# Up projection of a gated MLP: the convolution's sum in PSUM, the gelu further back in ScalarE's queue, the residual on every second tile

## The chip, the cores and the metric

The kernel runs on one core of a Trainium2 chip. The metric is the device time of one execution in microseconds. Engines are named as in the profile: PE is TensorE (PEld its weight loads), DVE is VectorE, ACT is ScalarE, POOL is GpSimd, SP is SyncE, which here only issues transfers. PSUM has eight banks of 128 x 512 fp32; matmuls write there, and DVE and ACT can read and write there too.

## The reference, cut to what matters

One decoder layer on 512 tokens of width 2048: attention heads of four kinds, an output projection, a layer norm, and a gated MLP with a second layer norm. The change concerns the MLP's first half:

```python
def conv_ffn(x, w_up, conv_w, conv_b, w_down):
    S = x.shape[1]
    u, g = jnp.split(x @ w_up, 2, axis=-1)
    gp = jnp.pad(g, ((0, 0), (CONV_WIDTH - 1, 0), (0, 0)))
    gc = conv_b
    for tap in range(CONV_WIDTH):
        gc = gc + conv_w[tap] * gp[:, tap:tap + S]
    return (jax.nn.gelu(gc) * u) @ w_down
...
    h = layer_norm(DEEPNORM_ALPHA * h + mix, ln1_g[l], ln1_b[l])
    ffn = conv_ffn(h, ffn_w_up[l], ffn_conv_w[l], ffn_conv_b[l], ffn_w_down[l])
    h = layer_norm(DEEPNORM_ALPHA * h + ffn, ln2_g[l], ln2_b[l])
```

The hidden width is 5632, that is 44 tiles of 128 hidden columns (f = 0 to 43), each with 512 tokens on the free axis.

## The kernel before

Everything is fp32, and each product is made from three matmuls on rounded parts (high x high, high x low, low x high, in the code `PARTS`). The up projection (`ffn_up`) multiplies blocks in Strassen's manner with seven products: a tile f takes two **units** of weights (u = 0 and 1, each half of the 2048 rows), and a unit is 7 products x 4 blocks x 3 parts = 84 matmuls of 128 x 256. A tile's results lie in four PSUM banks `bk[0..3]`; even tiles take three banks of a ring of three and one of a ring of five, odd tiles four of the ring of five. Tile 0 is made in another way, and the last two tiles take their units in another order.

Each unit's operands are prepared ahead of PE by `weight_operands`, called by `next_unit`:

- SP loads the raw weights `wr` (L918, two transfers of 512 KB, four buffers).
- ACT writes `wl` = -raw (L925) and `wh` = rounded raw (L928). `wh` and `wl` have two buffers each, so both wait until PE has done the first three of the seven products of the unit two before.
- POOL issues an accumulating transfer (L926, 768 KB) that adds the raw weights from memory to `wl`, which leaves raw minus rounded. PE needs `wl` at the very start of the unit.
- POOL makes four sums of blocks, `S` (L934 to L937); ACT rounds each (L899) and DVE takes the rest (L900, the pair in `split_pair`). PE needs these `ws` from the fourth product on.

Once a tile's second unit is through, `up_finish` (L988 on) collects the banks: ACT copies `bk[0]`, whose first half alone is used (L995), DVE makes the gate `g` and the other half `up` (L996 to L1002). `gated` then makes the convolution: ACT the last tap and the bias (L1010), DVE the two others (L1011, L1013) into an SBUF tile `c`, ACT the gelu in place (L1015), POOL the product with `up` (L1016). After every odd tile `set_aside` has POOL make three or four half sums `ht` (L1031 to L1036) and SP store all to memory. Once a tile, on 16 tiles in a row (f = 2 to 17), `up_residual` loads a piece of the first norm's output, multiplies and adds on DVE (L1054, L1055), and stores it for the end of the down projection.

The order of the instructions on each engine is set at compile time by a scheduler from the order of the code and from priorities: all of `weight_operands` is moved ahead by a priority of 900. On the chip each engine takes its instructions strictly in that order, and so does SP with its transfers. SBUF temporaries (`tmp`) come from a ring of 36.

Of the kernel before, what the change touches and what calls it, by code (L numbers as in the profile page):

```python
# [13 lines left out]
AF = mybir.ActivationFunctionType  # L14
# [7 lines left out]
NT = S // P  # L22
NMEM = 256
DFF = 5632
FT = DFF // P
# [16 lines left out]
class Trunk:  # L42
    def __init__(self, ctx, tc, x, memt, wfg, wm, wmkv, wout, wup, wdown, wtail, w1, prm, rows,
                 out):
        self.tc, self.nc = tc, tc.nc
        self.x, self.memt, self.wfg, self.wm, self.wmkv = x, memt, wfg, wm, wmkv
        self.wout, self.wup, self.wdown, self.wtail, self.w1 = wout, wup, wdown, wtail, w1
        self.prm_d, self.rows, self.out = prm, rows, out
        pool = lambda name, bufs, **kw: ctx.enter_context(tc.tile_pool(name=name, bufs=bufs, **kw))
        self.pT = pool("pT", 16)  # L50
        self.pW = pool("pW", 3)
        self.pP = pool("pP", 2)
        self.pt = pool("pt", 36)
        self.sm = pool("sm", 3)
        self.cst = pool("cst", 1)
        self.ps = pool("ps", 4, space=bass.MemoryType.PSUM)
        self.dram = pool("dram", 1, space=bass.MemoryType.DRAM)
        self.wm_next = 0

        self.queue = deque()  # L60
        self.stage_b, self.stage_c = deque(), deque()
        self.phase = 0
        self.every, self.count = 24, 0
        self.late = deque()
        self.ahead = 0
        self.unit, self.unit_no = None, 0

# [828 lines left out]


    def split_pair(self, raw, h, l):
        self.nc.scalar.copy(h, raw)  # L899
        self.nc.vector.tensor_sub(l, raw, h.bitcast(F32))  # L900

    def next_unit(self):

        w = self.unit
        self.unit = self.weight_operands(self.units.popleft()) if self.units else None
        self.unit_no += 1
        return w

    def weight_operands(self, src):

        nc = self.nc
        with self.tc.high_priority(offset=900 if self.unit_no > 1 else 200):
            raw = [self.pW.tile([P, 2, 512], F32, tag="wr", name="wr", bufs=4) for _ in range(2)]
            for p in range(2):
                nc.sync.dma_start(raw[p], src[:, 2 * p:2 * p + 2])  # L918
            a21, a11 = raw[0][:, 0], raw[0][:, 1]
            a12 = raw[1][:, 0]  # L920
            a22 = raw[1][:, 1]
            h3, l3 = (self.pW.tile([P, 3, 512], F32R, tag=g, name=g, bufs=2)
                      for g in ("wh", "wl"))
            for o, i in ((slice(0, 1), raw[0][:, 1:2]), (slice(1, 3), raw[1])):
                nc.scalar.mul(l3[:, o], i, -1.0)  # L925
            nc.gpsimd.dma_start(l3, src[:, 1:4], accum_op=ALU.add)  # L926
            for o, i in ((slice(0, 1), raw[0][:, 1:2]), (slice(1, 3), raw[1])):
                nc.scalar.copy(h3[:, o], i)  # L928
            if self.unit_no < 2:
                w = [self.tmp("w21", dt=F32R, tag="w") for _ in range(2)]  # L930
                self.split_pair(a21, *w)
                return [[h3[:, i], l3[:, i]] for i in range(3)] + [w]
            s12, s34 = (self.pP.tile([P, 2, 512], F32, tag="P", name="S") for _ in range(2))
            nc.gpsimd.tensor_add(s12[:, 0], a21, a22)  # L934
            nc.gpsimd.tensor_sub(s12[:, 1], s12[:, 0], a11)  # L935
            nc.gpsimd.tensor_sub(s34[:, 0], a11, a21)  # L936
            nc.gpsimd.tensor_sub(s34[:, 1], a12, s12[:, 1])  # L937
            ws = []
            for t in (s12, s34):
                for i in range(2):  # L940
                    ws.append([self.tmp("ws", dt=F32R, tag="w") for _ in range(2)])
                    self.split_pair(t[:, i], *ws[-1])
        return [[h3[:, i], l3[:, i]] for i in range(3)] + ws


# [42 lines left out]
    def up_finish(self, f, bk):  # L988
        nc = self.nc
        half = lambda ap: ap.rearrange("p (a n) -> p a n", a=2)  # L990

        pu = half(self.tmp("pu"))
        p1, u2 = pu[:, 0], pu[:, 1]
        g, uu = self.tmp("g"), self.tmp("uu", (P, 2, 256))
        nc.scalar.copy(p1, bk[0][:, :256])  # L995
        nc.vector.tensor_add(u2, p1, bk[1][:, 256:])  # L996
        nc.vector.tensor_add(g[:, :256], p1, bk[1][:, :256])
        nc.vector.tensor_add(uu, u2.unsqueeze(1).to_broadcast([P, 2, 256]), half(bk[2]))
        nc.vector.tensor_add(g[:, 256:], uu[:, 0], bk[3][:, :256])
        up = self.tmp("up")  # L1000
        nc.vector.tensor_add(up[:, :256], uu[:, 1], bk[3][:, 256:])
        nc.vector.tensor_add(up[:, 256:], uu[:, 1], bk[2][:, :256])  # L1002
        self.gated(f, g, up)

    def gated(self, f, g, up):

        nc = self.nc
        c = self.tmp("c")
        cw = lambda k: self.prm[:, C_CW + 44 * k + f:C_CW + 44 * k + f + 1]
        nc.scalar.activation(c, g, AF.Identity, bias=self.prm[:, C_CB + f:C_CB + f + 1], scale=cw(2))  # L1010
        nc.vector.scalar_tensor_tensor(c[:, 1:], g[:, :511], cw(1), c[:, 1:], op0=ALU.mult,  # L1011
                                       op1=ALU.add)
        nc.vector.scalar_tensor_tensor(c[:, 2:], g[:, :510], cw(0), c[:, 2:], op0=ALU.mult,  # L1013
                                       op1=ALU.add)
        nc.scalar.activation(c, c, AF.Gelu_apprx_tanh)  # L1015
        (nc.vector if f == 0 else nc.gpsimd).tensor_mul(c, c, up)  # L1016
        c = c.rearrange("p (a n) -> p a n", a=2)
        if f % 2 == 0:
            self.b1 = c
        else:  # L1020
            self.aside.append(self.set_aside(self.b1, c))
# [24 lines left out]
    def up_residual(self, i):  # L1046

        nc = self.nc
        n, t = divmod(i, NT)
        if t == 0:  # L1050
            self.gb1 = self.bc_row(2, n, "g1"), self.bc_row(3, n, "b1")
        a = self.tmp("res")
        nc.sync.dma_start(a, self.res[t][n])
        nc.vector.scalar_tensor_tensor(a, a, ALPHA, self.gb1[0], op0=ALU.mult, op1=ALU.mult)  # L1054
        nc.vector.scalar_tensor_tensor(a, self.gb1[1], ALPHA, a, op0=ALU.mult, op1=ALU.add)  # L1055
        self.res[t][n] = self.dram.tile([P, 512], F32, name=f"ares{t}{n}")
        nc.sync.dma_start(self.res[t][n], a)

# [108 lines left out]
    def ffn(self):  # L1169
        nc = self.nc  # L1170
# [3 lines left out]
        for f, u in self.up_sequence():  # L1174
            n = int(f in seen)
            seen.add(f)
            if f > 0:
                self.ffn_up(f, u, n)
            elif n:
                self.gated(f, *self.up_first())  # L1180
            if n and 2 <= f < 18:
                self.up_residual(f - 2)
        self.st2 = [self.cst.tile([P, 4, 6], F32, name=f"st2_{t}") for t in range(NT)]
        self.due = deque((4, 5))
        acc = []
# [1 line left out]
        for c, k0, nk in self.CHUNKS:  # L1187
            sets = self.column_sets(c)
            for q in sets:
                bk = [self.bank("g" if i < 3 else "a", "dn") for i in range(7)]  # L1190
                nu = nk // 2
                for u in range(nu):
                    w = self.next_unit()
# [26 lines left out]
        for f in range(2, 4):  # L1220
            h, l = self.load_unit(self.wtail[f])
            tail += [(h[:, k * 512:(k + 1) * 512], l[:, k * 512:(k + 1) * 512]) for k in range(2)]
        gb = [(self.bc_row(4, q, "g2"), self.bc_row(5, q, "b2")) for q in range(4)]
# [164 lines left out]
```

## Time and profile before

| | us |
|---|---|
| median of 3 runs | 2334.61 |
| lowest and highest | 2327.23, 2335.04 |
| the profiled execution | 2341.35 |
| its span, first to last instruction | 2339.6 |
| mean granted clock of PE, share of full speed | 0.983 |
| PE busy | 2232.7 |
| DVE, ACT, POOL busy | 1591.7, 1229.5, 1368.4 |

The up projection lies at 945 to 1815 us of the span, the down projection behind it. Busy time says how full an engine is, not whether it is waited for; for that the waits of PE are read by stretch, and then who held up the one that PE waited for.

### The profile page before, as it was taken

How to read it: one execution, taken by the hardware profiler on the slowest of the kernel's cores; microseconds unless marked ns; L12 is line 12 of the kernel's file. 1: busy time of each engine (PE TensorE's matmuls, PEld its weight loads, DVE VectorE, ACT ScalarE, POOL GpSimd, SP SyncE). 2: the span in 40 equal slices, each digit the busy share in tenths (PEclk: the TensorE clock that was granted, in tenths of full speed). 3: DMA queues.
4: the chain of work that ended last, by engine and by line, in shares of the span. 5: the costliest groups of instructions: out<-in, count | busy, mean ns of one | idle time of the engine just before them, and what ended most of it. 6: DMA issues, size and time to landing. Idle time of an engine off the chain costs nothing. (4 is left out here: it accounts for less than half of the span.)

```text
span 2339.6 us, 40306 instructions
## 1 busy us (share of the span) xinstructions
PE 2232.7 (95%) x15454; PEld 2083.5 (89%) x15454; DVE 1591.7 (68%) x2204; ACT 1229.5 (53%) x2129; POOL 1368.4 (58%) x1197
## 2 busy tenths in 40 slices
PE   7999999999999998899999999999999899999995
PEld 6788888888888878899999999999999899899994
DVE  7544455456675348687787767777676878677778
ACT  5444453355563135565555555565555666565651
POOL 5212110123234517787887878877777687777874
PEclk9999999999999999999999999999999999999998
DMA  6322223222124363888888777777778888788873
GB/s 228 92 81 73 78 67 106 84 64 62 59 88 149 104 188 94 224 226 227 231 222 238 202 210 207 201 204 197 212 202 227 243 241 233 193 229 216 207 191 115
DMA packets 125362, 392.75 MB, mean 168 GB/s; under 512 B 13632, under 2 KB 23744, under 8 KB 125168
## 3 DMA queue, kind: packets, MB, share of 16 engines
q1 hardware_dynamic: 106304, 287.72, 35.6%
q0 software_dynamic: 18720, 102.24, 24.6%
q8 instruction: 121, 1.98, 0.3%
q14 instruction: 73, 0.60, 0.1%
q10 hardware_dynamic: 144, 0.21, 0.0%
HBM read 354.36 MB, written 35.65 MB: 167 GB/s over the span
## 5 line engine op out<-in xcount | busy, mean ns | idle before, releaser
L900 DVE TENSOR_TENSOR ws<-S,ws 128x512 fp32r<-128x512 f32 x512 | 600.1, 1192 | 244.3 <-ACT ws L899 238.9
L963 PE MATMUL up<-xt,ws 128*128 128x256 f32 x3096 | 386.4, 283 | 0.3 <-DVE ws L900 0.3
L963 PEld LDWEIGHTS up<-xt,ws 128*128 128x128 f32 x3096 | 378.0, 192 | 0.6 <-DVE ws L900 0.6
L899 ACT CAST ws<-S 128x512 fp32r<-128x512 f32 x512 | 307.0, 615 | 114.9 <-POOL S L934 33.5
L100 DVE TENSOR_TENSOR wl<-wr,wh 128x1024 fp32r<-128x1024 f32 x122 | 155.2, 1272 | 213.3 <-ACT wh L99 198.4
L936 POOL TENSOR_TENSOR S<-wr 128x512 f32<-128x512 f32 x128 | 212.0, 1656 | 92.5 <-DVE ws L900 87.3
L342 POOL TENSOR_SCALAR P<-P,r 128x128 f32<-128x128 f32 (+3 forms) x144 | 81.1, 582 | 308.5 <-DVE r L337 166.2
L963 PE MATMUL up<-x,wh 128*128 128x256 f32 x1376 | 258.8, 288 | 0.0
L99 ACT CAST wh<-wr 128x1024 fp32r<-128x1024 f32 x122 | 128.0, 1049 | 233.7 <-PE op L733 78.8
L934 POOL TENSOR_TENSOR S<-wr 128x512 f32<-128x512 f32 x128 | 183.8, 1436 | 108.0 <-issue 45.3
L925 ACT ACTIVATE wl<-wr 128x512 fp32r<-128x512 f32 (+1 forms) x260 | 205.1, 836 | 67.3 <-PE dn L1115 43.5
L928 ACT CAST wh<-wr 128x512 fp32r<-128x512 f32 (+1 forms) x260 | 211.5, 829 | 35.7 <-PE up L963 33.8
L963 PE MATMUL up<-x,wl 128*128 128x256 f32 x688 | 200.8, 292 | 29.5 <-DMA wl<-in_wup_dram 29.3
L963 PEld LDWEIGHTS up<-x,wh 128*128 128x128 f32 x1376 | 220.5, 197 | 0.0
L937 POOL TENSOR_TENSOR S<-wr,S 128x512 f32<-128x512 f32 x128 | 211.8, 1655 | 0.0
L935 POOL TENSOR_TENSOR S<-S,wr 128x512 f32<-128x512 f32 x128 | 198.5, 1551 | 9.7
L1115 PE MATMUL dn<-wh,hx 128*128 128x256 f32 x792 | 157.5, 292 | 13.3 <-DVE acc L1128 8.6
L963 PEld LDWEIGHTS up<-x,wl 128*128 128x128 f32 x688 | 135.8, 197 | 33.7 <-DMA wl<-in_wup_dram 33.7
L1115 PEld LDWEIGHTS dn<-wh,hx 128*128 128x128 f32 x792 | 132.3, 200 | 14.9 <-issue 6.3
L733 PE MATMUL op<-wh,oTs 128*128 128x512 f32 x448 | 140.6, 391 | 0.0
L963 PE MATMUL up<-x,ws 128*128 128x256 f32 x1032 | 137.9, 283 | 0.0
L1015 ACT ACTIVATE c<-c 128x512 f32<-128x512 f32 x44 | 27.8, 632 | 208.0 <-DVE c L1013 208.0
(327 smaller groups left out, 5321.3 us busy)
## 6 DMA issues: line engine op xcount, KB each, us to landing
wr<-in_wup_dram SPq DMA_DIRECT2D x176, 512.0 KB
wl<-in_wup_dram POOLq DMA_DIRECT2D x88, 768.0 KB, 7.5
wr<-in_wm_dram SPq DMA_DIRECT2D x84, 512.0 KB
wr<-in_wdown_dram SPq DMA_DIRECT2D x84, 512.0 KB
wl<-in_wdown_dram POOLq DMA_DIRECT2D x42, 768.0 KB, 7.4
wr<-in_wout_dram SPq DMA_DIRECT2D x32, 512.0 KB
hid<-c SPq DMA_DIRECT2D x44, 256.0 KB
hid<-ht SPq DMA_DIRECT2D x44, 256.0 KB
```

What stands on the lines that cost most here:

```text
L100: nc.vector.tensor_sub(l[:, :cols], raw[:, :cols], h[:, :cols].bitcast(F32))
L733: nc.tensor.matmul(ps, ot[ct][:, a, t * P:(t + 1) * P], w[b][:, c2 * 512:(c2 + 1) * 512], start=(first and (a, b) == (0, 0)), stop=(last a ...
L899: self.nc.scalar.copy(h, raw)
L900: self.nc.vector.tensor_sub(l, raw, h.bitcast(F32))
L925: nc.scalar.mul(l3[:, o], i, -1.0)
L928: nc.scalar.copy(h3[:, o], i)
L934: nc.gpsimd.tensor_add(s12[:, 0], a21, a22)
L935: nc.gpsimd.tensor_sub(s12[:, 1], s12[:, 0], a11)
L936: nc.gpsimd.tensor_sub(s34[:, 0], a11, a21)
L937: nc.gpsimd.tensor_sub(s34[:, 1], a12, s12[:, 1])
L963: self.nc.tensor.matmul(ps, w[iw][i][:, k * P:(k + 1) * P], x[j][ix], start=(opens and k == 0 and (i, j) == (0, 0)), stop=(last and k == 3 ...
L1115: self.nc.tensor.matmul(bk[i][:, a * 256:(a + 1) * 256], x[ix][j][:, a * P:(a + 1) * P], w[iw][p][:, q * 256:(q + 1) * 256], start=first a ...
```

## The change

Three things, all in the up projection:

1. For f = 1 to 41 the convolution is summed in `bk[0]`, the bank that held the first product, and not in an SBUF tile. (For tile 0, 42 and 43 all stays as it was.)
2. For the same tiles the gelu, its product with `up` and what follows are put off to the next call of `next_unit` (`defer`, `run_deferred`), and the gelu is queued on ACT behind the last rounding of the unit prepared by that call (`issue_after(self.mark.ins)` orders the queue only). The gelu's result goes to a new SBUF tile.
3. `up_residual` runs on every second tile from f = 2 to 32, and each piece is loaded when the piece before has been stored.

```diff
     def split_pair(self, raw, h, l):
-        self.nc.scalar.copy(h, raw)
+        ins = self.nc.scalar.copy(h, raw)
         self.nc.vector.tensor_sub(l, raw, h.bitcast(F32))
+        return ins
+
+    def defer(self, units, work):
+        self.deferred.append((self.unit_no + units, work))
+
+    def run_deferred(self):
+        todo = [w for n, w in self.deferred if n < self.unit_no]
+        self.deferred = [d for d in self.deferred if d[0] >= self.unit_no]
+        with self.tc.issue_after(self.mark.ins):
+            for work in todo:
+                work()
 
     def next_unit(self):
 
         w = self.unit
         self.unit = self.weight_operands(self.units.popleft()) if self.units else None
         self.unit_no += 1
+        self.run_deferred()
         return w
...
-                    self.split_pair(t[:, i], *ws[-1])
+                    self.mark = self.split_pair(t[:, i], *ws[-1])
...
-        self.gated(f, g, up)
+        self.gated(f, g, up, bk[0] if f < FT - 2 else None)
...
-    def gated(self, f, g, up):
+    def gated(self, f, g, up, c=None):
         nc = self.nc
-        c = self.tmp("c")
+        if c is None:
+            c = self.tmp("c")
...
-        nc.scalar.activation(c, c, AF.Gelu_apprx_tanh)
+        if 0 < f < FT - 2:
+            self.defer(0, lambda: self.activate(f, c, up))
+        else:
+            self.activate(f, c, up)
+
+    def activate(self, f, s, up):
+        nc = self.nc
+        c = self.tmp("c") if 0 < f < FT - 2 else s
+        nc.scalar.activation(c, s, AF.Gelu_apprx_tanh)
         (nc.vector if f == 0 else nc.gpsimd).tensor_mul(c, c, up)
...
     def up_residual(self, i):
         nc = self.nc
+        def load(i):
+            n, t = divmod(i, NT)
+            gb = (self.bc_row(2, n, "g1"), self.bc_row(3, n, "b1")) if t == 0 else None
+            a = self.tmp("res")
+            nc.sync.dma_start(a, self.res[t][n])
+            return a, gb
         n, t = divmod(i, NT)
-        if t == 0:
-            self.gb1 = self.bc_row(2, n, "g1"), self.bc_row(3, n, "b1")
-        a = self.tmp("res")
-        nc.sync.dma_start(a, self.res[t][n])
+        a, gb = self.res_next if i else load(i)
+        self.gb1 = gb or self.gb1
...
         nc.sync.dma_start(self.res[t][n], a)
+        if i + 1 < 4 * NT:
+            self.res_next = load(i + 1)
...
-            if n and 2 <= f < 18:
-                self.up_residual(f - 2)
+            if n and 2 <= f < 34 and f % 2 == 0:
+                self.up_residual(f // 2 - 1)
```

How the queues move. ACT, in the middle of the up projection, from the last roundings of one unit to the copy of the next tile's first bank (L928, L925, L899 prepare units; L1010 is the first tap, L1015 the gelu, L995 the copy). Before:

```order
L1010 ACTIVATE c<-g,prm 128x512
L1015 ACTIVATE c<-c 128x512
L928 CAST wh<-wr 128x512
L925 ACTIVATE wl<-wr 128x512
L925 ACTIVATE wl<-wr 128x1024
L899 CAST ws<-S 128x512
L928 CAST wh<-wr 128x1024
L899 CAST ws<-S 128x512 x3
L995 COPY pu<-up 128x256
```

After the change (the same lines are L1026, L1039, L942, L939, L899, L1009; `up` is here the bank):

```order
L1026 ACTIVATE up<-g,prm 128x512
L942 CAST wh<-wr 128x512
L939 ACTIVATE wl<-wr 128x512
L939 ACTIVATE wl<-wr 128x1024
L899 CAST ws<-S 128x512
L942 CAST wh<-wr 128x1024
L899 CAST ws<-S 128x512
L1039 ACTIVATE c<-up 128x512
L899 CAST ws<-S 128x512 x2
L1009 COPY pu<-up 128x256
```

The gelu has gone back by six instructions: the next `wh` and `wl` and two roundings now stand ahead of it.

POOL, after an odd tile, where the half sums are made (L934 to L937 sum blocks, L1016 is the product with `up`, L926 issues the transfer to `wl`). Before:

```order
L934 TENSOR_TENSOR S<-wr 128x512
L935 TENSOR_TENSOR S<-S,wr 128x512
L1031 TENSOR_TENSOR ht<-c 128x256
L1016 TENSOR_TENSOR c<-c,up 128x512
L1032 TENSOR_TENSOR ht<-c,ht 128x256
L1035 TENSOR_TENSOR ht<-c 128x256
L1036 TENSOR_TENSOR ht<-c,ht 128x256
L926 DMA wl<-in_wup_dram 128x1536
L936 TENSOR_TENSOR S<-wr 128x512
L937 TENSOR_TENSOR S<-wr,S 128x512
```

After the change (the same lines are L948, L949, L1055, L1040, L1056, L1059, L1060, L940, L950, L951):

```order
L948 TENSOR_TENSOR S<-wr 128x512
L949 TENSOR_TENSOR S<-S,wr 128x512
L940 DMA wl<-in_wup_dram 128x1536
L1055 TENSOR_TENSOR ht<-c 128x256
L1040 TENSOR_TENSOR c<-c,up 128x512
L950 TENSOR_TENSOR S<-wr 128x512
L951 TENSOR_TENSOR S<-wr,S 128x512
L1056 TENSOR_TENSOR ht<-c,ht 128x256
L1059 TENSOR_TENSOR ht<-c 128x256
L1060 TENSOR_TENSOR ht<-c,ht 128x256
L948 TENSOR_TENSOR S<-wr 128x512
L949 TENSOR_TENSOR S<-S,wr 128x512
```

The transfer to `wl` has moved ahead of the product and the half sums; these now stand ahead of the transfer of the unit after.

## Rows read from the trace of the kernel before

**Rows 1.** The page, part 1: busy us (share of the span) xinstructions
```profile
PE 2232.7 (95%) x15454; PEld 2083.5 (89%) x15454; DVE 1591.7 (68%) x2204; ACT 1229.5 (53%) x2129; POOL 1368.4 (58%) x1197
```
**Rows 2.** PE's waits in 965:1795, 1795:1815 and 945:955: total, times, longest us
```profile
PE up L963 <- DMA wl<-in_wup_dram: 19.3, 18, 4.5
...
PE up L963 <- DMA wl<-in_wup_dram: 4.5, 1, 4.5
...
PE up L963 <- DMA wl<-in_wup_dram: 5.6, 1, 5.6
```
**Rows 3.** Windows: PE, PEld, DVE, ACT, POOL busy us; PEclk, DMA share, GB/s
```profile
1095.00:1115.00 20.00, 18.73 (x137) 18.73 (x138) 12.47 (x13) 9.72 (x16) 14.25 (x12) 0.84 0.90 239
...
1265.00:1290.00 25.00, 23.89 (x177) 23.89 (x178) 17.55 (x21) 12.88 (x20) 18.16 (x15) 0.86 0.91 245
...
1795.00:1900.00 105.00, 92.07 (x708) 90.68 (x707) 81.99 (x88) 62.02 (x107) 70.38 (x54) 0.93 0.90 258
```
**Rows 4.** Timeline of PE at three unit starts: start us, us, instruction, [wait]
```profile
1535.58 0.40 PE L963 MATMUL up<-x,wh 128*128 128x256 f32 x2
...
1545.66 0.40 PE L963 MATMUL up<-x,wh 128*128 128x256 f32 x2
...
1555.74 0.40 PE L963 MATMUL up<-x,wh 128*128 128x256 f32 x2
1556.60 0.39 PE L963 MATMUL up<-x,wl 128*128 128x256 f32 x1 [0.46 <-DMA wl<-in_wup_dram]
```
**Rows 5.** Timeline of ACT, 1539 to 1549 us, after an odd tile
```profile
1539.48 0.82 ACT L1010 ACTIVATE c<-g,prm 128x512 f32<-128x512 f32 x1 [3.16 <-DVE g L999]
1544.15 0.63 ACT L1015 ACTIVATE c<-c 128x512 f32<-128x512 f32 x1 [3.85 <-DVE c L1013]
1544.68 0.60 ACT L928 CAST wh<-wr 128x512 fp32r<-128x512 f32 x1
1545.19 1.58 ACT L925 ACTIVATE wl<-wr 128x512 fp32r<-128x512 f32 x2
1546.67 0.60 ACT L899 CAST ws<-S 128x512 fp32r<-128x512 f32 x1
1547.18 1.04 ACT L928 CAST wh<-wr 128x1024 fp32r<-128x1024 f32 x1
```
**Rows 6.** Timeline of POOL, 1541 to 1557 us, the same place
```profile
1541.89 1.62 POOL L935 TENSOR_TENSOR S<-S,wr 128x512 f32<-128x512 f32 x1
1544.86 1.30 POOL L1016 TENSOR_TENSOR c<-c,up 128x512 f32<-128x512 f32 x1 [1.35 <-ACT c L1015]
...
1548.76 0.87 POOL L926 DMA_DIRECT2D wl<-in_wup_dram  x1
1549.56 1.67 POOL L936 TENSOR_TENSOR S<-wr 128x512 f32<-128x512 f32 x1
1551.19 1.74 POOL L937 TENSOR_TENSOR S<-wr,S 128x512 f32<-128x512 f32 x1
...
1554.72 1.62 POOL L935 TENSOR_TENSOR S<-S,wr 128x512 f32<-128x512 f32 x1
1556.29 0.86 POOL L926 DMA_DIRECT2D wl<-in_wup_dram  x1
```
**Rows 7.** Line L926 in 945:1815, all 82 transfers: from issue to landing
```profile
DMA to landing us min/median/max: 6.5/7.4/11.7
```
**Rows 8.** Waits of ACT and of DVE in 945:1815: total us, times, longest
```profile
ACT c L1015 <- DVE c L1013: 205.2, 41, 6.7
...
DVE res L1054 <- DMA res<-res: 49.1, 15, 5.2
```
**Rows 9.** Timelines of DVE and POOL: the convolution's tap at two places
```profile
1542.39 1.67 DVE L1013 SCALAR_TENSOR_TENSOR c<-g,prm,c 128x510 f32<-128x510 f32 x1
...
932.33 0.74 DVE L1011 SCALAR_TENSOR_TENSOR c<-up,prm,c 128x511 f32<-128x511 f32 x1
...
931.81 1.75 POOL L937 TENSOR_TENSOR S<-wr,S 128x512 f32<-128x512 f32 x1
```

More of the change, by code (lines that the diff above doesn't have):

```diff
@@ L63, in __init__ @@
         self.every, self.count = 24, 0
-        self.late = deque()
+        self.late, self.deferred = deque(), []
         self.ahead = 0
@@ L930, in weight_operands @@
                 w = [self.tmp("w21", dt=F32R, tag="w") for _ in range(2)]
-                self.split_pair(a21, *w)
+                self.mark = self.split_pair(a21, *w)
                 return [[h3[:, i], l3[:, i]] for i in range(3)] + [w]
```

## The prediction

> **What bounds the kernel now.** Three views were read, from the whole down to one transfer. First the page's busy times: PE is busy 95% of the span, no other engine over 68% [rows 1]. So time is to be had only where PE stands still or runs at a lower clock; a busy engine elsewhere matters only through whom it makes late. Next the waits of PE in the up projection, by stretch: in 965 to 1795 us it waits for one thing alone, the transfer that completes a unit's `wl`, 18 times, 19.3 us in all, 4.5 at the longest; the same wait stands once before that stretch (5.6 us) and once behind it (4.5) [rows 2]. The windows add the clock: behind the two longest waits of the stretch the granted clock is 0.84 over 20 us and 0.86 over 25 us [rows 3]. Of its two levels, 2.4 and 1.2 GHz, PE had part of those windows at the lower, just after it had stood idle.
>
> Then one late transfer is followed back, at 1556.60, where PE waits 0.46 us for `wl` [rows 4]. The transfer was issued at 1548.76 [rows 6]. Ahead of it on POOL stand the product with `up` (1544.86 to 1546.16, having waited for the gelu) and three half sums (the 2.6 us up to 1548.76); S's two sums, the last thing it needs on POOL, were done at 1541.89 + 1.62 = 1543.51 [rows 6]. ACT was no better: the gelu was queued right behind the first tap and held ACT 3.85 us for DVE's last tap, so the negated weights, which the transfer adds to, came only at 1545.19 to 1546.77 [rows 5]. Over the whole stage ACT spends 205.2 us in that one wait, 5.0 us for each of 41 tiles; DVE spends 49.1 us waiting for residual pieces [rows 8].
>
> **The change part by part.**
>
> *Gelu further back.* No instruction is added; ACT's rows are put in a new order. Behind the first tap, which ends at 1539.48 + 0.82 = 1540.30 [rows 5], ACT now goes on at once with L928 (0.60) and L925 (1.58): negated weights at 1542.5. POOL's sums end at 1543.5, and the transfer now stands right behind them: issue at 1543.5 and not 1548.8, 5.3 us earlier. The longest PE wait in the stage's middle is 4.5 us [rows 2], so if all late transfers move by as much, all 18 waits go: 19.3 us. With them goes the clock they cost: 20 x (1 - 0.84) + 25 x (1 - 0.86) = 3.2 + 3.5 = 6.7 us [rows 3]. Together **26.0 us**.
>
> What is late next? The product and the half sums are only moved, and now stand ahead of the following unit's transfer. ACT reaches the gelu after L899 (0.60), L928 (1.04) and another L899 (0.60) [rows 5], at 1542.5 + 2.2 = 1544.7; DVE's last tap ended at 1542.39 + 1.67 = 1544.06 [rows 9], so the gelu finds its data and waits for nobody. Then POOL: gelu's end 1545.4, product 1.30, L936 and L937 1.67 + 1.74, half sums 2.6, L934 and L935 1.62 each [rows 6]: issue at 1556.0. Before, that transfer went out at 1556.29 [rows 6]. PE's units follow each other by 10.08 us (1535.58, 1545.66, 1555.74 [rows 4]) and take `wl` with their third matmul, so PE wants it at 1566.1. At the median landing of 7.4 us it is there at 1563.4, 2.7 us early; at the longest, 11.7 us, it is 1.6 late [rows 7]. So a few short waits may be left.
>
> *The sum in a bank.* DVE's two taps and the gelu read, ACT's first tap and DVE write in PSUM. No PE bank is missed: `bk[0]` of tile f is wanted again by tile f + 2, two units (20.2 us) after f is through, and the gelu that frees it ends about 9.8 us after f's end (1545.4 against 1535.6, where the next unit starts [rows 4]). For the price of a tap the bounds are 0.74 us, where the one input lay in a bank, while POOL was at work on L937, and 1.67 us with both inputs in SBUF [rows 9]. I take 0.74, since the new form too has one input in PSUM and one in SBUF. The Trainium skill, "SBUF — State Buffer", section "Who interferes with whom", says that a DVE instruction with two SBUF inputs contends with a GpSimd instruction that reads SBUF, and one with a single SBUF input does not; by that rule the tap would cost the lower bound. The two rows agree with it. Either way some 41 x 2 x 0.93 = 76 us of DVE's time is off PE's path: worth 0 directly. If it did not come about, the gelu would wait 0, as worked out with 1.67.
>
> *The residual on every second tile, loaded ahead.* The same 16 pieces, 32 transfers and 32 DVE instructions. DVE's 49.1 us of waits go, since each load has two tiles' time; behind them DVE's rests (L900) come earlier, and with them POOL's L936. PE does not wait for these, so again 0 directly. The loads and stores move from the first half of the stage into the whole. On SP the store of a piece still stands ahead of later weight loads, as before; at no cost, as long as DVE is less late than it was.
>
> *Ends of the stage.* The 5.6 us at its start hang on tile 0, which keeps its old order: 0. The 4.5 us near its end hang on the last deferred tile; that transfer moves up too. But PE is idle 105.0 - 92.1 = 12.9 us over 1795 to 1900 [rows 3], for other reasons as well (the first hidden tiles come back from memory, DMA share 0.90), so half of it, **2.2 us**, is counted.
>
> Sum: 26.0 + 2.2 = 28.2 us off 2341.35, the time of the profiled execution. That one is 6.7 us above the median of the runs, 2334.61; part of its waits may not be in ordinary runs. If all of the 6.7 were such waits the gain would be 21.5; I take the middle, 24.8, off the median: **2310 us**.
>
> **The rivals.**
>
> *A: the transfer starts earlier and takes longer.* The stage's transfers keep the DMA queues at shares of 0.84 to 0.91 around the long waits [rows 3], and landing stretches from 6.5 to 11.7 us [rows 7]. If an earlier start meets the raw loads and half of the 5.3 us is given back in landing, the waits under 2.6 us still go and the two long ones, with their clock, stay in part: about half, 12 us, 2323. Against it: the bytes stay the same and the median is 7.4, far from the worst. The Trainium skill, "Trainium Kernel Development and Optimization", section "Key Constraints", says that DMAs from the SP, ACT and POOL queues all run on the same 16 engines and interleave, and that issuing from several only saves issue time. By that rule this rival could well decide; the trace shows the spread of landing, not its cause.
>
> *B: the change does not do what it says.* The wait that ACT loses turns up on POOL, at the product, or the gelu still waits for the taps, and `wl` stays late for lack of anything faster in front of it: 2335. For it: POOL's L934 and L935 themselves take a wait before 1541.89. Against it: the order shows the transfer ahead of product and half sums.
>
> *C: slower.* The unit after an odd tile gets the late transfer instead. Its margin is 2.7 us. The place is POOL's product, which now stands ahead of four sums, three half sums and the transfer; each us by which the gelu is later than 1544.7 moves the issue by one. There are about 20 such pairs of tiles. With 26 us won and 20 us paid for each us beyond the margin, it turns at a gelu 2.7 + 1.3 = 4.0 us later than worked out. If the gelu came 5.0 us late, as long as it waits on average now [rows 8], PE would lose 20 x 2.3 = 46 us and win 26: 2355. Against it: all that stands ahead of the gelu on ACT is ready by then.
>
> **How the numbers follow.** Half a per cent, 11.7 us, is about what a measurement of this kernel can tell from no change. The forecast has 0.67, and its own range is 2300 to 2321 (all 28.2 us and the start of the stage with its clock; 13 us as the least). A has 0.14, half of it on either side of the limit at 2323; B 0.12; C 0.07. Faster: 0.67 x 0.97 + 0.07 = 0.72. Same: 0.02 + 0.07 + 0.12 = 0.21. Slower: 0.07. The range for 8 in 10 goes from 2298 to 2331: it takes in A and part of B and leaves out C.
>
> **What would show it.** In the changed kernel's profile: PE's waits for `wl` in the up projection under 10 us in all, not 29; ACT's wait for DVE's last tap near 0, not 205; the transfer to `wl` after an odd tile issued right behind L935 and 7 to 8 us into PE's unit, not 13; taps at about 0.74 us; no DVE wait for residual pieces; a clock of 1.00 between the stage's ends. I am wrong if PE's waits for `wl` stay while the gelu's wait is gone (A, or B if POOL is the one in front), or if PE waits for `wl` in the other unit of the pair (C).

## The result, and the profile after

The changed kernel takes 2313.95 us (median of 6 runs, 2310.99 to 2321.85) against 2333.22 us of the kernel before beside it (6 runs): a ratio of 0.9918, with a 95% interval of 0.99 to 0.9937. Forecast were 2310 us and a range of 2298 to 2331. The profiled execution has a span of 2314.3 us (before 2339.6) and a mean granted clock of 0.985 (before 0.983). The number came out as forecast, in part by luck: half of the account behind it did not hold, as the experiments below show.

The waits of PE in the up projection, 965 to 1795 us, of the changed kernel (line, what is waited for: us in total, times, longest), against 19.3 us in 18 waits [rows 2]:

```profile
PE up L977 <- DMA wl<-in_wup_dram: 1.5, 1, 1.5
PE up L977 <- DVE ws L900: 0.6, 1, 0.6
```

And in 945 to 965 us, where the forecast left the first wait alone:

```profile
PE up L977 <- DMA wl<-in_wup_dram: 5.8, 1, 5.8
```

The windows (PE, PEld, DVE, ACT, POOL busy us, then PE clock, DMA share, GB/s) show PE from 965 us on almost without a gap (2.1 us idle in all) and at the upper level, 2.4 GHz, up to the stage's end, and then a hole:

```profile
965.00:1095.00 130.00, 130.00 (x1086) 130.00 (x1085) 93.68 (x115) 77.97 (x123) 99.80 (x82) 1.00 0.89 232
1095.00:1265.00 170.00, 170.00 (x1419) 170.00 (x1419) 119.02 (x141) 102.81 (x162) 132.08 (x108) 1.00 0.88 229
1265.00:1795.00 530.00, 527.89 (x4397) 527.49 (x4396) 374.15 (x430) 316.44 (x494) 419.99 (x339) 1.00 0.86 221
1795.00:1900.00 105.00, 82.62 (x635) 81.52 (x634) 76.93 (x87) 59.43 (x101) 68.51 (x50) 0.89 0.79 220
```

Before, the long waits inside the stage had windows at 0.84 and 0.86, and 1795 to 1900 had 92.07 us of PE at 0.93 [rows 3]. Now that last window has 82.62 us at 0.89.

POOL after an odd tile, in the timeline of the changed kernel (start, us, instruction, idle before and what ended it):

```profile
1398.42 1.29 POOL L949 TENSOR_TENSOR S<-S,wr 128x512 f32<-128x512 f32 x1
1399.65 0.89 POOL L940 DMA_DIRECT2D wl<-in_wup_dram  x1
1400.26 1.05 POOL L1055 TENSOR_TENSOR ht<-c 128x256 f32<-128x256 f32 x1
1401.48 1.55 POOL L1040 TENSOR_TENSOR c<-c,up 128x512 f32<-128x512 f32 x1 [0.16 <-ACT c L1039]
...
1411.43 0.87 POOL L940 DMA_DIRECT2D wl<-in_wup_dram  x1
```

and PE at the same place:

```profile
1390.99 1.60 PE L977 MATMUL up<-x,ws 128*128 128x256 f32 x12
```

The 12 matmuls start 0.12 us apart, so the unit ends 1.44 us on, at 1392.43, and the transfer goes out 7.2 us into the next unit. Before, it was 1548.76 against a unit start of 1535.58, 13.2 us [rows 4, 6]. It stands right behind the sums, ahead of product and half sums, as forecast. The taps now take 742 and 753 ns (column behind the busy time), against 1.67 us [rows 9]:

```profile
L1029 DVE SCALAR_TENSOR_TENSOR up<-g,prm,up 128x510 f32<-128x510 f32 x41 | 30.9, 753 | 1.4
L1027 DVE SCALAR_TENSOR_TENSOR up<-g,prm,up 128x511 f32<-128x511 f32 x41 | 30.4, 742 | 0.0
```

ACT's wait for the last tap fell from 205.2 us [rows 8] to 4.6. But DVE waits longer for the residual pieces, not less, 75.4 us against 49.1 [rows 8] (waits in 945 to 1815):

```profile
DVE res L1084 <- DMA res<-res: 75.4, 15, 11.0
```

And behind the stage stand new waits of PE, in 1795 to 1900:

```profile
PE dn L1147 <- ACT pu L1009: 10.5, 1, 10.5
PE dn L1147 <- ACT hx L899: 9.2, 2, 7.9
PE dn L1147 <- DVE g L1011: 2.4, 1, 2.4
PE dn L1147 <- DVE hx L900: 0.4, 1, 0.4
```

The first of them, in ACT's timeline: the copy of tile 42's bank (L1009), which releases PE at 1808.87, stands behind a rounding that waits for a load and some twenty more instructions.

```profile
1788.68 0.61 ACT L899 CAST ws<-S 128x512 fp32r<-128x512 f32 x1
1796.80 0.62 ACT L899 CAST hx<-hx 128x512 fp32r<-128x512 f32 x1 [7.51 <-DMA hx<-hid]
...
1808.46 0.36 ACT L1009 COPY pu<-up 128x256 f32<-128x256 f32 x1
```

**Where the time went.** The up projection ends at 1798.4 us (1808.87 less the wait of 10.46) and not at 1829.6: 31.2 us earlier. Idle time of PE explains 21.7 of these, the clock and the rest 9.5. In the first 50 us of the down projection PE is idle for 22.4 us and not 6.5, so 15.9 are given back; later it is idle 7.6 us less, for reasons that were not followed up. 31.2 - 15.9 + 7.6 = 22.9, of 25.3 us between the two profiled executions.

### The profile page after: what moved, and what is told of

Read it like the earlier page. It is cut to its first block, busy times and chain, and to the rows that moved or that the text cites. A ratio compares the mean times of both kernels' runs of the same rounds, so it can differ in the third digit from the quotient of the medians.

```text
span 2314.3 us, 40352 instructions
## 1 busy us (share of the span) xinstructions
PE 2219.9 (96%) x15454; PEld 2074.7 (90%) x15454; DVE 1540.9 (67%) x2204; ACT 1234.5 (53%) x2129; POOL 1334.1 (58%) x1197
## 5 line engine op out<-in xcount | busy, mean ns | idle before, releaser
L900 DVE TENSOR_TENSOR ws<-S,ws 128x512 fp32r<-128x512 f32 x512 | 618.1, 1225 | 245.4 <-ACT ws L899 239.2
L899 ACT CAST ws<-S 128x512 fp32r<-128x512 f32 x512 | 313.9, 614 | 130.7 <-PE up L977 56.1
L942 ACT CAST wh<-wr 128x512 fp32r<-128x512 f32 (+1 forms) x260 | 212.0, 831 | 128.9 <-PE up L977 126.9
L950 POOL TENSOR_TENSOR S<-wr 128x512 f32<-128x512 f32 x128 | 203.7, 1591 | 102.0 <-DVE ws L900 97.8
L977 PE MATMUL up<-x,wh 128*128 128x256 f32 x1376 | 253.3, 284 | 0.0
L99 ACT CAST wh<-wr 128x1024 fp32r<-128x1024 f32 x122 | 128.0, 1050 | 233.1 <-PE op L733 73.8
L948 POOL TENSOR_TENSOR S<-wr 128x512 f32<-128x512 f32 x128 | 178.4, 1393 | 118.8 <-issue 82.2
L939 ACT ACTIVATE wl<-wr 128x512 fp32r<-128x512 f32 (+1 forms) x260 | 205.1, 836 | 76.7 <-PE dn L1147 56.4
L951 POOL TENSOR_TENSOR S<-wr,S 128x512 f32<-128x512 f32 x128 | 211.6, 1653 | 0.0
L977 PE MATMUL up<-x,wl 128*128 128x256 f32 x688 | 196.0, 285 | 7.4 <-DMA wl<-in_wup_dram 7.4
L949 POOL TENSOR_TENSOR S<-S,wr 128x512 f32<-128x512 f32 x128 | 186.5, 1457 | 9.8
L1147 PE MATMUL dn<-ws,hx 128*128 128x256 f32 x1044 | 133.2, 284 | 0.7 <-DVE acc L1160 0.7
```

Source lines behind the costliest of these rows:

```text
L899: ins = self.nc.scalar.copy(h, raw)
L977: self.nc.tensor.matmul(ps, w[iw][i][:, k * P:(k + 1) * P], x[j][ix], start=(opens and k == 0 and (i, j) == (0, 0)), stop=(last and k == 3 ...
L1147: self.nc.tensor.matmul(bk[i][:, a * 256:(a + 1) * 256], x[ix][j][:, a * P:(a + 1) * P], w[iw][p][:, q * 256:(q + 1) * 256], start=first a ...
```

## The experiments

The change has three parts: the sum in the bank, the deferral of gelu and product, and the residual on every second tile. All eight combinations were run. The idle times of PE are added up from the trace, over 965 to 1300 us, 1300 us to the end of the up projection, and the first 50 us of the down projection, from one profiled execution each; "up ends" is in the span. Ratios are to the kernel before on the same chip, whose median was 2335.3, 2336.9 and 2331.9 us beside the three groups of runs, and 2333.2 beside the change itself (last row).

| bank | deferral | spread | median, us | ratio (95%) | idle to 1300 | idle to end | up ends | idle, 50 us of down |
|---|---|---|---|---|---|---|---|---|
| - | - | - | before | 1 | 11.5 | 12.3 | 1829.6 | 6.5 |
| yes | - | - | 2313.22 | 0.9881 (0.9855 to 0.9907) | 5.1 | 2.6 | 1806.0 | 5.3 |
| - | yes | - | 2343.2 | 1.0042 (1.0017 to 1.0068) | 20.1 | 0.3 | 1826.6 | 21.7 |
| - | - | yes | 2340.15 | 1.0012 (0.9996 to 1.0028) | 8.4 | 16.4 | 1832.6 | 10.0 |
| yes | yes | - | 2342.51 | 1.0038 (1.0021 to 1.0054) | 18.5 | 1.5 | 1825.5 | 22.0 |
| yes | - | yes | 2304.86 | 0.9871 (0.9852 to 0.9891) | 3.9 | 1.0 | 1802.1 | 6.8 |
| - | yes | yes | 2315.23 | 0.992 (0.9901 to 0.9939) | 3.7 | 2.4 | 1801.7 | 20.4 |
| yes | yes | yes | 2313.95 | 0.9918 (0.99 to 0.9937) | 0.0 | 2.1 | 1798.4 | 22.4 |

Read in pairs, the rows show that no part has a worth of its own. The deferral takes time off only beside the spread without the bank (1.0012 to 0.992, about 21 us); alone and beside the bank it adds 0.004 to 0.016. The bank takes 0.0119 to 0.0141 off without the deferral and nothing beside it (1.0042 and 1.0038, 0.992 and 0.9918). The spread takes about 0.012 off with the deferral and nothing measurable without it.

**Without the deferral** (all else as in the change):

```diff
-        if 0 < f < FT - 2:
-            self.defer(0, lambda: self.activate(f, c, up))
-        else:
-            self.activate(f, c, up)
+        self.activate(f, c, up)
```

> The changed kernel with the gelu, product and half sums back in their old place in the queues; the sum in the bank and the new residual stay. Theory (order): the late wl transfer came from ACT, where the gelu stood ahead of the negation, and from POOL, where product and half sums stood ahead of the transfer. The shorter taps bring gelu and product forward by about 2 x 0.93 = 1.9 us, so the transfer after an odd tile goes out 1.9 and not 5.3 us earlier than before: PE's waits for wl over the up projection 8 to 14 us (19.3 before, 1.5 after), time 2321 to 2328 us. Rival (taps): what mattered was the length of the taps, not the order: waits under 4 us, time near that of the change, 2314. Rival (residual): the spread residual did it: also near 2314.

Measured: 2304.86 us, under the change, and the intervals of the two ratios lie apart. PE's waits for `wl` in 965 to 1795 are 4.8 us. So the part that the prediction credited with the whole gain costs about half a per cent beside the two others. Of the expectations, those of the two rivals came nearest.

**Without the bank** (deferral and spread stay; `gated` sums in SBUF):

```diff
-        self.gated(f, g, up, bk[0] if f < FT - 2 else None)
+        self.gated(f, g, up)
```

> The changed kernel with the convolution summed in SBUF as before; gelu still put off, new residual. Theory (order): taps back at 1.6 to 1.7 us, which is off PE's path; the put-off gelu finds its data all the same; PE's waits for wl under 4 us, time 2314 plus or minus 4. Rival (taps): waits for wl back to 10 us and more, time 2325 or above.

Measured: 2315.23 us, as the theory expected, with 4.0 us of waits for `wl` in 965 to 1795 (under 4 was said). The taps are back at the old price; nothing but the place of the sum was changed:

```profile
L1027 DVE SCALAR_TENSOR_TENSOR c<-g,prm,c 128x511 f32<-128x511 f32 x43 | 68.4, 1590 | 0.2 <-ACT c L1026 0.2
```

**With the old residual** (bank and deferral stay):

```diff
-            if n and 2 <= f < 34 and f % 2 == 0:
-                self.up_residual(f // 2 - 1)
+            if n and 2 <= f < 18:
+                self.up_residual(f - 2)
```

> The changed kernel with the residual as before (one piece on each of 16 tiles in a row, loaded when used). Theory (order): DVE's wait for residual pieces goes from 75 us back to about 50, nobody on PE's path sees it: time 2314 plus or minus 4. Rival (residual): spreading the pieces took load off SP, POOL and DVE in the first half of the stage: PE's waits for wl come back in 1000 to 1400 us, time 2320 or above. A third possibility: the longer waits of DVE and SP in the changed kernel cost something at the stage's end: then 2305 to 2310.

Measured: 2342.51 us, slower than before, ratio 1.0038. The rival was right, and by more than it had said. PE's waits in 965 to 1300 us:

```profile
PE up L977 <- DMA wl<-in_wup_dram: 10.7, 6, 3.0
PE up L977 <- DVE ws L900: 7.7, 2, 4.0
```

One of these is followed back. PE waits 3.01 us for `wl` at 1152.87. On DVE, ahead of it:

```profile
1134.58 0.69 DVE L1078 SCALAR_TENSOR_TENSOR res<-res,g 128x512 f32<-128x512 f32 x1 [6.59 <-DMA res<-res]
1135.30 0.69 DVE L1079 SCALAR_TENSOR_TENSOR res<-b,res 128x512 f32<-128x512 f32 x1
1135.91 5.29 DVE L900 TENSOR_TENSOR ws<-S,ws 128x512 fp32r<-128x512 f32 x5
```

and on POOL:

```profile
1130.25 1.58 POOL L1040 TENSOR_TENSOR c<-c,up 128x512 f32<-128x512 f32 x1
1137.28 1.67 POOL L950 TENSOR_TENSOR S<-wr 128x512 f32<-128x512 f32 x1 [5.45 <-DVE ws L900]
1138.91 1.74 POOL L951 TENSOR_TENSOR S<-wr,S 128x512 f32<-128x512 f32 x1
1140.61 1.18 POOL L1056 TENSOR_TENSOR ht<-c,ht 128x256 f32<-128x256 f32 x1
...
1142.46 1.19 POOL L1060 TENSOR_TENSOR ht<-c,ht 128x256 f32<-128x256 f32 x1
1143.60 1.29 POOL L948 TENSOR_TENSOR S<-wr 128x512 f32<-128x512 f32 x1
1144.97 1.30 POOL L949 TENSOR_TENSOR S<-S,wr 128x512 f32<-128x512 f32 x1
1146.21 0.87 POOL L940 DMA_DIRECT2D wl<-in_wup_dram  x1
```

DVE stands 6.59 us before a residual piece that has not landed. Its rests of the rounded weights are behind that, POOL's third sum waits for them, and behind the sum stand three half sums (3.0 us, 1140.61 to 1143.60) and then the next transfer. With the gelu in its old place the half sums are through before POOL comes to this wait: in the run with the bank alone, below, they end at 1121.9 us and the wait at the third sum ends at 1125.3, with the transfer issued in between. In 945 to 1300 us DVE waits 89.5 us for pieces, POOL 73.8 us for DVE, and SP 122.2 us to store pieces.

**The product alone put off** (gelu, sum and residual as before):

```diff
+        nc.scalar.activation(c, c, AF.Gelu_apprx_tanh)
         if 0 < f < FT - 2:
             self.defer(0, lambda: self.activate(f, c, up))
...
-        nc.scalar.activation(c, s, AF.Gelu_apprx_tanh)
         (nc.vector if f == 0 else nc.gpsimd).tensor_mul(c, c, up)
```

> The kernel before with one thing: the product with up and the half sums put off behind the next unit's roundings, the gelu itself in its old place on ACT, sum in SBUF, old residual. So POOL's queue is as in the change, ACT's as before. Theory (order, both engines): the transfer can go no earlier than the negation behind the gelu, 1546.8 in the unit followed, against 1548.8 before and 1543.5 with the change: 2 of 5.3 us, so waits for wl of 9 to 15 us and a time of 2322 to 2329. If POOL's queue alone was the cause: waits under 4, 2314. If ACT's queue alone: waits near 19, 2333.

Measured: 2332.86 us, ratio 0.9993 (0.9979 to 1.0008). The edit did nothing: from 965 to 1790 us POOL takes its instructions in the order of the kernel before, one by one. `issue_after` binds ACT's queue only, and ACT has no part in what was put off; the scheduler left the rest where it was. In this run:

```profile
1500.22 1.62 POOL L949 TENSOR_TENSOR S<-S,wr 128x512 f32<-128x512 f32 x1
1503.19 1.30 POOL L1040 TENSOR_TENSOR c<-c,up 128x512 f32<-128x512 f32 x1 [1.35 <-ACT c L1031]
...
1507.10 0.88 POOL L940 DMA_DIRECT2D wl<-in_wup_dram  x1
```

So it tells ACT's queue from POOL's no better than before; that question stays open.

**The bank alone** (the kernel before, with the sum in `bk[0]`):

```diff
-        self.gated(f, g, up)
+        self.gated(f, g, up, bk[0] if f < FT - 2 else None)
...
-        c = self.tmp("c")
+        if c is None:
+            c = self.tmp("c")
...
+        c = self.tmp("c") if 0 < f < FT - 2 else s
+        nc.scalar.activation(c, s, AF.Gelu_apprx_tanh)
```

> The kernel before with one thing: the convolution summed in the bank. Gelu and all behind it in the old place, residual as before. The run without the deferral gave 2304.9, 30 us under before; this and the next run divide that. If the bank alone did it (taps 0.75 instead of 1.65 us, so gelu, product and the wl transfer 1.9 us earlier after each odd tile): 2305 to 2310, waits of PE for wl in 965 to 1795 under 6 us. If the two parts add: the second half of the stage, where the residual never ran, loses its 7.7 us of waits, the first half keeps most of its 11.5: 2315 to 2326. If the residual alone did it: 2330 or above.

Measured: 2313.22 us, ratio 0.9881, between the first two cases: the bank alone is worth 24 to 28 us (the medians differ by 23.7; 0.0119 x 2337 = 27.8). ACT still waits for the last tap, 117.3 us over the stage and not 205.2. But POOL no longer waits for the gelu at the product: 0.3 us in all, against this line of the kernel before (945 to 1815):

```profile
POOL c L1016 <- ACT c L1015: 38.1, 35, 1.4
```

After an odd tile, POOL and PE:

```profile
1528.59 1.19 POOL L1057 TENSOR_TENSOR ht<-c,ht 128x256 f32<-128x256 f32 x1
1529.72 0.87 POOL L940 DMA_DIRECT2D wl<-in_wup_dram  x1
```

```profile
1517.70 1.60 PE L977 MATMUL up<-x,ws 128*128 128x256 f32 x12
```

The unit begins at 1517.70 + 1.44 = 1519.14, so the transfer goes out 10.6 us into it, still behind product and half sums: 2.6 us earlier than before. With 7.7 us of landing, this run's median, it is there at 18.3. PE wants it at 20.6, with the third matmul of the unit after next (1556.60 less its wait of 0.46, against 1535.58 [rows 4]). Before, 13.2 + 7.4 [rows 7] = 20.6: on time by nothing at the median, and late whenever landing took longer. The place is a typical one: over the odd tiles of 965 to 1790 us the transfer goes out at the median 6.6 us ahead of the unit that uses it before, and 9.6 us ahead with the bank. So some 3 us is nearly all that was missing. The 6.0 us of the change are more than PE can use.

**The spread alone, and without the early load.** First the kernel before with the new residual only, then bank and spread with each piece loaded when used:

```diff
-        a, gb = self.res_next if i else load(i)
+        a = self.tmp("res")
+        nc.sync.dma_start(a, self.res[t][n])
...
-        if i + 1 < 4 * NT:
-            self.res_next = load(i + 1)
```

> The kernel before with one thing: the residual on every second tile from 2 to 32, each piece loaded when the piece before has been stored. If the residual alone did it: 2305 to 2310. If the parts add: the first half's waits for wl fall from 11.5 to 4 to 7 us, the second half's stay near 8 or grow a little, since half of the pieces are there now: 2315 to 2326. If the bank alone did it: 2330 or above.

> The sum in the bank, no deferral, the residual on every second tile but each piece loaded when it is used, as before. Theory: the load ahead never came about, since its buffer comes free late and SP takes it just before DVE wants it; so this equals the run without the deferral, 2305 plus or minus 4, with DVE's wait for the pieces near 59 us in both. Rival: what is left of the early load counts: 2312 or above, DVE's waits for the pieces 80 us or more.

Measured: 2340.15 us (ratio 1.0012) and 2307.61 us (0.987, 0.9848 to 0.9891). The spread alone moves waits from the first half into the second (8.4 and 16.4 us) and wins nothing, as was said for the case that the bank alone did it. The load ahead is worth nothing measurable: with it and without it bank and spread come to the same ratio, and DVE waits 58.6 and 55.2 us for the pieces over the stage.

**Store the piece later.** The run with the old residual (1.0038), each piece's store two tiles later and behind weight loads on SP:

```diff
-        nc.sync.dma_start(self.res[t][n], a)
+        self.res_done = getattr(self, 'res_done', []) + [(self.res[t][n], a)]
...
+            if n and 4 <= f < 20:
+                with self.tc.issue_after(self.loaded.ins):
+                    self.nc.sync.dma_start(*self.res_done.pop(0))
```

> The run with the old residual (2342.5, bank and deferral in) with one thing: each piece's store to memory put off by two tiles and queued on SP behind the weight loads. Theory (SP): with the deferral the store stands on SP right behind its own load, SP stands 122 us in 15 such waits, and the raw weight loads behind it come late, so that sums, roundings and wl are late. Then SP's wait goes to under 20 us, PE's waits in 965 to 1300 from 18 us to under 7, and the time falls by 15 to 28 us, to 2315 to 2327. Rival (DVE): it is DVE's own wait for the piece (90 us) that delays its rests of the rounded weights; it stays, and the time stays at 2336 or above.

Measured: 2355.14 us, ratio 1.0068 (1.0047 to 1.0089) against 1.0038: no faster. SP's 122.2 us for the stores are gone, but DVE's wait for the pieces is not (96.4 us), and SP stands elsewhere instead: about 57 us longer for POOL's product, to store `c`, and 63 us longer for POOL's sums, ahead of the weight loads (102.6 us in the run it was made from):

```profile
SPq L932 <- POOL S L950: 165.8, 29, 12.2
```

The theory that SP's stores were the cause has fallen: without them SP gets to the weight loads no sooner. The rival, DVE, was left.

**Scale the piece later.** The same run again; DVE scales a piece behind the rests of the next unit, not in front of them:

```diff
+        self.piece = n, t, a
+
+    def scale_residual(self):
+        nc = self.nc
+        n, t, a = self.piece
+        with self.tc.issue_after(self.rest.ins):
...
+            if not n and 3 <= f < 19:
+                self.scale_residual()
```

> The run with the old residual (2342.5, bank and deferral in) with one thing: DVE scales each piece not right behind the tile's taps but behind the rests of the next unit's rounded weights, so that DVE does not stand in front of them waiting for the piece. Theory (DVE in order): DVE's wait for the piece (90 us) holds its rests, these hold POOL's third sum (73.8 us of waits), and behind that sum stand, with the deferral, the product and the half sums and then the next wl transfer. Then DVE's wait for pieces falls under 40 us, POOL's for the rests under 45, PE's waits in 965 to 1300 from 18 to under 7, time 2314 to 2328. Rival: the wait is only moved, since the piece's load stands on SP behind weight loads that wait for the same sums: PE's waits stay over 14 us, 2336 or above.

Measured: 2316.67 us, ratio 0.9932 (0.9909 to 0.9956) against 1.0038. PE waits for nothing at all in 965 to 1795. POOL's waits for DVE in 945 to 1300 fell from 73.8 us to

```profile
POOL S L950 <- DVE ws L900: 8.8, 10, 1.6
```

and DVE's for the pieces from 89.5 to 38.8. Each store goes back with the scaling, but that alone, in the run before this one, had won nothing. That a wait of DVE for data which nobody needs soon reaches PE through the order of DVE's queue is shown. That the half sums are what makes it reach further with the deferral is read from the rows above; it was not tried by itself.

**The deferral alone** (from the change: sum in SBUF, the residual as before and loaded when used):

```diff
-        self.gated(f, g, up, bk[0] if f < FT - 2 else None)
+        self.gated(f, g, up)
...
-            if n and 2 <= f < 34 and f % 2 == 0:
-                self.up_residual(f // 2 - 1)
+            if n and 2 <= f < 18:
+                self.up_residual(f - 2)
```

> The kernel before with the deferral alone: sum in SBUF, residual as before. Theory: the deferral takes the gelu out of ACT's way and wins in the second half of the stage (7.7 us of waits to under 3), but in the first half, where a piece comes on every tile, it puts half sums and product behind POOL's wait for DVE and wins nothing or loses, and at the end of the stage it costs some 10 us: 2334 to 2346. Rival, the prediction's own account (the deferral makes the whole gain, bank and residual are worth nothing): 2310 to 2316.

Measured: 2343.2 us, slower than before. The second half's idle time goes from 12.3 to 0.3 us, the first half's from 11.5 to 20.1, and the start of the down projection has 21.7 for 6.5. The prediction's account, by which this part carries everything, is out.

**Collect tile 42 earlier.** The change, with hidden tiles 2 and 3 later in the program and the roundings of tiles 2 to 5 behind the two copies on ACT (`self.collected` is the copy):

```diff
-            for kp in range(4):
+            for kp in range(2):
                 self.hidden_operands(kp)
...
+        if (f, n) == (FT - 2, 1):
+            for kp in range(2, 4):
+                self.hidden_operands(kp)
...
+        late = 2 <= kp < self.SLOTS
+        with self.tc.high_priority(offset=ahead), \
+                self.tc.issue_after(self.collected.ins) if late else nullcontext():
```

> The changed kernel with one thing at the stage's end: the hidden tiles 2 and 3 of the down projection are loaded and rounded after the collection of up tile 42 in the program, and ACT's roundings for tiles 2 to 5 are queued behind the copies of tiles 42 and 43's first banks. Theory: PE's 10.5 us wait at the start of the down projection is for a copy whose bank was complete 20 us before, behind roundings that wait for loads; the copy goes first, PE's wait falls to 0 to 3 us, some of it comes back at the second hidden pair: 2303 to 2310. Rival: PE would wait for the hidden tiles just as long: 2312 to 2317.

Measured: 2307.06 us, ratio 0.9894 (0.9873 to 0.9915). That is 0.0024, some 6 us, under the change, but the two intervals overlap. In the trace the wait for the copy is gone; the hidden tiles take part of its place (1795 to 1850):

```profile
PE dn L1152 <- ACT hx L899: 5.8, 1, 5.8
PE dn L1152 <- DMA wl<-in_wdown_dram: 3.4, 1, 3.4
PE dn L1152 <- DVE hxt L900: 3.2, 2, 1.8
```

The idle time of the first 50 us of the down projection is 14.6 and not 22.4 us. The order of these loads and roundings is thus worth about 8 us in the profile; over the runs it is not shown. It comes with the deferral: the four combinations with it have 20 to 22 us there, the four without it 5 to 10.

**A version meant to beat both:** bank and spread, no deferral, pieces scaled behind the rests (edits as above).

> A version meant to beat both: sum in the bank, no deferral, a piece on every second tile, loaded when used, and scaled by DVE behind the next unit's rests. Theory: PE's waits for wl in the stage under 3 us as in the run with the spread alone (1.5), DVE's wait for pieces from 55 to under 25 us, off PE's path: 2301 to 2309. Rival: the longer life of the pieces or their later stores hold weight loads on SP: 2312 or above.

Measured: 2303.75 us, ratio 0.987 (0.9848 to 0.9891). PE waits for nothing in 965 to 1795, and DVE's waits for pieces are 5.3 us. It beats both kernels, by about 28 us (medians) and 11 us (0.0048 x 2333). It can't be told from bank and spread alone (0.9871 and 0.987): the few us left in the stage were all there was to win.

## Why the prediction was right, and where it was not

- **What bounds the kernel.** Right. The waits for `wl`, followed back from PE, and the clock behind them were where time was to be had: the up projection ends 31.2 us earlier, where 28.2 were counted.
- **Gelu further back, 26.0 us.** The place and the time of the transfer came out (7.2 us into the unit, 7 to 8 said), the waits went, the clock is 1.00. But as the cause of the gain the step failed. It asked by how much the transfer moves (5.3 us) and not by how much it was late. The bank alone moves it 2.6 us, and takes 0.0119 off the time; the deferral on its own makes the kernel slower, and only beside the spread without the bank does it take time off (0.0092, about 21 us). Either makes `wl` early enough where no piece is in the way, and both together win no more. The step "what is late next?" looked at the following unit's transfer on POOL with every wait at zero. It did not put in POOL's wait for DVE at L936, which now stands ahead of the half sums and was there in the kernel before (945 to 1815):

```profile
POOL S L936 <- DVE ws L900: 56.8, 33, 3.9
```

- **The bank, worth 0.** The price was right (0.74 and 0.75 us; 1.59 in SBUF when only the place was changed). The Trainium skill, "SBUF — State Buffer", section "Who interferes with whom", says that a DVE instruction with two SBUF inputs contends with a GpSimd instruction that reads SBUF. The trace agrees, and more clearly than the prediction's two rows, which were both taken with POOL at work. With both inputs in SBUF but POOL idle (from 973.55 to 975.44 us) the tap takes 0.74 us in the kernel before too:

```profile
974.03 0.74 DVE L1013 SCALAR_TENSOR_TENSOR c<-g,prm,c 128x510 f32<-128x510 f32 x1
```

So what the bank buys here is not a faster place for the sum, but that the taps no longer slow down while POOL works; POOL's second sum is shorter with it as well (1592 and 1360 ns on average in 965 to 1795). The worth of 0 was right beside the deferral, as it was counted (0.9918 and 0.992). Its reason was wrong: the 76 us were called off PE's path either way, though the same text had followed the path through them: `wl` waits for the negation and the product, these for the gelu, the gelu for the taps. Without the deferral the bank takes 0.0119 off.

- **The residual, worth 0.** Wrong twice. DVE's waits did not go, they grew to 75.4 us: each piece is loaded just before its use all the same (SP issues the last load at 1539.61 us, and DVE stands 4.25 us for it, up to 1547.05). And with the deferral they are not off PE's path. With bank and deferral the old residual costs some 28 us (0.0120 x 2333); "PE does not wait for these" held only as long as nothing for PE stood behind them.
- **The ends of the stage, 2.2 us.** The start stayed, as said (5.6 and 5.8). At the end the sign was wrong: 15.9 us of new idle time. PE was counted up to the last unit of the stage, and not beyond, to what it wants next: a copy that ACT's order puts behind some twenty instructions and a load.
- **The sum.** 28.2 counted and 24.8 taken; the median fell by 19.3 and the profiled execution by 25.3. The stage gave more than counted (31.2), the start of the down projection took back 15.9 that were not counted at all, and later 7.6 came in that nobody had looked for. These errors have opposite signs, and the allowance for the profiled execution's distance from the median covered the rest: that the total came out is partly luck.
- **The rivals.** A is out: landing is 6.5, 7.3 and 11.0 us (least, median, most) with a DMA share of 0.86 to 0.89, against 6.5, 7.4 and 11.7 [rows 7]. B is out: the transfer did move ahead, and the waits went. C, slower through POOL's queue, did not decide in the change, but its mechanism is that of the runs with the deferral and the old residual, with the wait of POOL for DVE as the place and not the gelu.

## What to carry to other kernels

Ask of a late transfer how late it is before asking how much earlier it can go: here about 3 us did nearly all, and the 6 us of the change were paid for elsewhere. When work is put off on a queue, look for the longest wait that it now stands behind, on that queue and past the end of the stage, and not only for what it stood in front of. And a forecast that holds says little of its reasons until its parts have been run apart.

## What was not expected of the hardware

The prediction had not looked at how a tap with both inputs in SBUF depends on POOL: it takes 1.67 us while POOL works and 0.74 us while POOL is idle, the same as with one input in a bank. What surprised was how far one wait reaches: the 15 stops of SP for its stores, 122.2 us in all, gave nothing back when they were taken away (the ratio was 1.0068 for 1.0038, and SP stood as long elsewhere), while 50.7 us less of DVE's waits for the same pieces (89.5 to 38.8) gave some 25 us (0.0106 x 2333).
